# Two-layer decoder trunk on one core: background steps admitted by an account of VectorE's columns, a second W tile in PSUM, rotations and late gates on GpSimd

## The chip, the cores and the metric

The kernel runs on one core of a Trainium2 chip. The metric is the device time of one execution in microseconds; here the median of the runs shown. One execution was profiled; its trace gives the rows below.

## What is computed

Two decoder layers over 256 positions of width 2048, in float32, followed by an RMSNorm. Each layer normalizes its input, projects it with one wide matrix, runs several kinds of attention side by side (layer 0: latent attention with 8 heads, block-sparse attention with 8, attention into 256 memory tokens with 4; layer 1: sliding-window attention with sinks, 16 heads, dilated attention with 6, memory attention with 4), gates the concatenated heads with SiLU, projects back and adds the residual. Layer 0, cut to what matters:

```python
h = rms_norm(x, norm_g) @ w_in
c_q, c_kv, k_pe, qkv_b, q_mem, gate = split_cols(h, EVEN_SPLITS)
q_a = (rms_norm(c_q, q_norm_g) @ w_uq).reshape(B, S, MLA_HEADS, MLA_NOPE + MLA_ROPE)
q_a = jnp.concatenate([q_a[..., :MLA_NOPE], apply_rope(q_a[..., MLA_NOPE:], MLA_ROPE)], axis=-1)
...
y = jnp.concatenate([o_a, o_b.astype(o_a.dtype), o_m.astype(o_a.dtype)], axis=-1) * jax.nn.silu(gate)
return x + (y @ w_out).astype(x.dtype)
```

`apply_rope` rotates pairs of a head's first columns by an angle that grows with the position: x1\*cos - x2\*sin and x1\*sin + x2\*cos. These are "the rotations" below.

## The kernel before

**The stream of weights.** All weight matrices are cut into 334 pieces of 128 x 1024 columns at most, in a fixed plan (`_plan`): groups with names such as qr, kn0, v0, qn0, gB0 in layer 0, p0 to p9 in layer 1, and wo00 to wo13 for the output projections. A piece is loaded by a DMA (`raw`), rounded on ScalarE into `hi` (L393), and VectorE computes `lo = raw - hi` (L398). TensorE then does three passes per product, x_hi\*w_hi, x_hi\*w_lo, x_lo\*w_hi (L539 to L541): twelve matmuls of 128 x 512 for a full piece, in two halves of six. `raw`, `hi` and `lo` are rings of four tiles each (`RB`, `HB`); `ensure` runs three pieces ahead. A group's result stands in two of four `mm` banks of PSUM.

**The background.** Everything else is written as Python generators that emit a few instructions and then yield: evacuation of a group's banks (`rows`, by L663 to L675) into two tiles `wide`, rotation there (`rope_rows`, L592 to L621), a transposed layout by VectorE's 32x32 transposes (`g_land`, L634) and a round trip through DRAM, splits of queries and keys, scores, softmax (`g_softmax`), probabilities scaled into the tile `W` (L831, L832, L857, L859), transposed (`g_turn`, L812) and sent through DRAM, the product with the values, and the gate (`g_finish` L747 when the gate is there first, `g_gate` L764 when the head was first: a late gate). Results of layer y are split into columns of bufB or bufA, the input of the output projection.

**What sets the order.** Each engine runs its queue in the order in which instructions were emitted. `step` emits one piece: half of its matmuls, the late `lo` split of the piece two ahead, one round of background, the other half, the `hi` of the piece three ahead, one more round. A round is `run_bg`: each active generator advances by one yield, so by as many instructions as that step has; new heads start at most each fourth round, with six at once at most.

```python
        for g in list(active):
            try:
                next(g)
            except StopIteration:
                active.remove(g)
```

The attention banks (`at`) are four, handed out in turn, `W` is one tile, `wide` two. When a new group needs an `mm` bank whose evacuation has not been emitted, `mmtile` emits the rest of it on the spot (`force`).

## Time and profile before

| | |
|---|---|
| median of 3 runs | 991.64 us (991.05 to 991.83) |
| the profiled execution | 990.85 us, of which the span of instructions 989.1 us |
| mean granted TensorE clock | 0.992 |
| TensorE matmul busy | 965.4 us (98%) |
| VectorE busy | 696.2 us (70%) |
| ScalarE busy | 574.4 us (58%) |
| GpSimd busy | 20.0 us (2%) |
| chain that ended last | TensorE 87%, VectorE 7%, ScalarE 3% |

The profiled execution's own time is its span and 1.8 us around it. Busy time is an average over the whole span; where an engine waits is read from the waits and from the stretches. The granted clock is a share of TensorE's full speed: 1.00 is its upper level of 2.4 GHz, 0.50 the lower one of 1.2 GHz.

### The profile page before, as it was taken

Reading aid. Unit: us, or ns where it says so; the run is one execution under the profiler, and the core shown is the slowest. Engines: PE = TensorE matmul, PEld = TensorE weight load, DVE = VectorE, ACT = ScalarE, POOL = GpSimd, SP = SyncE. Lnnn points to the kernel's source line nnn. Section 1 sums busy time; section 2 is a strip of 40 time slices with the busy share of each in tenths; the row PEclk is TensorE's granted clock in tenths of the full one; section 3 lists DMA queues with packets and bytes.
Section 4 is the critical chain, followed back from the end, with each engine's and each line's share of the span. In section 5 each row is a group of like instructions: output and inputs, shape, how many; then the busy total and the mean of one; then the engine's idle time right before and its main releaser. Section 6 shows DMA issues by size and latency. Waiting matters only on the chain.

```text
span 989.1 us, 13362 instructions
## 1 busy us (share of the span) xinstructions
PE 965.4 (98%) x4541; PEld 808.9 (82%) x4541; DVE 696.2 (70%) x1324; ACT 574.4 (58%) x1045; POOL 20.0 (2%) x27
## 2 busy tenths in 40 slices
PE   9999998999999999999999999999898999999996
PEld 7888787888888888888888888887686988898885
DVE  6646879888567657776657656877888776786743
ACT  7766656676545646655556444655665664564541
POOL 0001000000000000000000000000000000000310
PEclk9999998999999999999999999999999999999998
DMA  8888978897767677888978756777766887688832
GB/s 332 323 278 267 304 228 268 272 310 229 238 215 245 216 240 246 266 280 269 331 249 289 261 195 218 236 234 235 251 220 212 269 274 227 217 296 301 288 125 85
DMA packets 136691, 248.25 MB, mean 251 GB/s; under 512 B 38960, under 2 KB 80176, under 8 KB 136624
## 3 DMA queue, kind: packets, MB, share of 16 engines
q1 hardware_dynamic: 135904, 246.59, 75.4%
q10 hardware_dynamic: 720, 0.82, 0.2%
q8 instruction: 35, 0.57, 0.2%
q14 instruction: 32, 0.26, 0.1%
HBM read 216.05 MB, written 31.33 MB: 250 GB/s over the span
## 4 chain that ended last, share of the span: by engine, by line
PE 87%; DVE 7%; ACT 3%; DMA 1%; issue 1%; SPq 0%; POOL 0%; DVEq 0%; ACTq 0%
PE mm L540 27%; PE mm L539 27%; PE mm L541 26%; PE at L917 2%; DVE lo L398 2%; PE at L908 2%; ACT hi L393 1%; PE at L912 1%; PE mm L1499 1%; PE mm L1498 1%; PE mm L1497 1%; DMA big<-in_memT 1%; DVE e L606 1%; DVE big L634 1%; DMA raw<-in_wall 1%
## 5 line engine op out<-in xcount | busy, mean ns | idle before, releaser
L398 DVE TENSOR_TENSOR lo<-raw,hi 128x1024 fp32r<-128x1024 f32 (+3 forms) x329 | 393.8, 1201 | 188.7 <-ACT hi L393 187.6
L393 ACT ACTIVATE hi<-raw 128x1024 fp32r<-128x1024 f32 (+3 forms) x329 | 339.2, 1035 | 219.3 <-PE mm L541 171.8
L540 PE MATMUL mm<-lo,bufB 128*128 128x512 f32 (+1 forms) x680 | 264.7, 389 | 7.0 <-DVE lo L398 6.9
L539 PE MATMUL mm<-hi,bufB 128*128 128x512 f32 (+1 forms) x680 | 265.8, 391 | 4.3 <-ACT wide L587 3.9
L541 PE MATMUL mm<-hi,bufB 128*128 128x512 f32 (+1 forms) x680 | 263.7, 388 | 0.0
L540 PE MATMUL mm<-lo,bufA 128*128 128x512 f32 (+1 forms) x620 | 239.3, 386 | 2.5 <-DVE lo L398 2.5
L539 PE MATMUL mm<-hi,bufA 128*128 128x512 f32 (+1 forms) x620 | 239.9, 387 | 0.6 <-DVE wide L583 0.6
L541 PE MATMUL mm<-hi,bufA 128*128 128x512 f32 (+1 forms) x620 | 238.8, 385 | 0.0
L540 PEld LDWEIGHTS mm<-lo,bufB 128*128 128x128 f32 x680 | 129.2, 190 | 33.4 <-DVE lo L398 9.1
L539 PEld LDWEIGHTS mm<-hi,bufB 128*128 128x128 f32 x680 | 129.3, 190 | 29.8 <-ACT wide L587 4.1
L541 PEld LDWEIGHTS mm<-hi,bufB 128*128 128x128 f32 x680 | 129.0, 190 | 24.6
L540 PEld LDWEIGHTS mm<-lo,bufA 128*128 128x128 f32 x620 | 116.5, 188 | 25.7 <-DVE lo L398 3.8
L539 PEld LDWEIGHTS mm<-hi,bufA 128*128 128x128 f32 x620 | 116.4, 188 | 23.2 <-PE mm L541 1.0
L541 PEld LDWEIGHTS mm<-hi,bufA 128*128 128x128 f32 x620 | 116.4, 188 | 23.1
L799 ACT ACTIVATE P<-P,st 128x128 f32<-128x128 f32 x76 | 33.7, 445 | 19.9 <-DVE st L793 18.9
L634 DVE STREAM_TRANSPOSE big<-wide 128x512 f32<-128x512 f32 (+1 forms) x68 | 43.5, 677 | 0.0
L790 DVE CUSTOM_DVE_ANT_1 P<-at,lay 128x128 f32<-128x128 f32 x76 | 24.0, 353 | 25.3 <-PE at L908 25.2
L831 ACT ACTIVATE W<-P,st 128x256 f32<-128x256 f32 x38 | 19.1, 502 | 26.9 <-DVE P L812 19.5
L812 DVE STREAM_TRANSPOSE P<-W 128x384 f32<-128x384 f32 (+1 forms) x54 | 28.7, 531 | 1.7 <-ACT W L831 1.5
L556 ACT ACTIVATE spl<-big 128x128 fp32r<-128x128 f32 (+1 forms) x76 | 23.5, 353 | 6.3 <-PE at L908 6.3
L843 ACT ACTIVATE PT<-P 128x256 fp32r<-128x256 f32 x38 | 15.2, 408 | 17.6 <-PE at L917 14.7
L558 DVE TENSOR_TENSOR spl<-big,spl 128x128 fp32r<-128x128 f32 (+1 forms) x76 | 23.7, 350 | 1.6 <-ACT spl L556 1.5
(166 smaller groups left out, 678.5 us busy)
## 6 DMA issues: line engine op xcount, KB each, us to landing
raw<-in_wall SPq DMA_DIRECT2D x309, 512.0 KB, 4.4
wd<-big SPq DMA_DIRECT2D x32, 512.0 KB, 5.1
big<-wd SPq DMA_DIRECT2D x32, 512.0 KB, 5.2
pd<-P SPq DMA_DIRECT2D x38, 192.0 KB, 4.4
P<-pd SPq DMA_DIRECT2D x38, 192.0 KB, 4.4
raw<-in_wall SPq DMA_DIRECT2D x16, 384.0 KB, 4.2
raw<-in_wall SPq DMA_DIRECT2D x8, 320.0 KB, 3.3
big<-in_xT SPq DMA_DIRECT2D x4, 512.0 KB, 6.3
```

The costliest lines, as they stand in the source:

```text
L393: nc.scalar.activation(hi[:, c], raw[:, c], AF.Copy)
L398: nc.vector.tensor_tensor(lo[:, c], raw[:, c], hi[:, c].bitcast(F32), op=OP.subtract)
L539: nc.tensor.matmul(p, xh, hi[:, w], start=kt == 0, stop=False, skip_group_check=True)
L540: nc.tensor.matmul(p, xh, lo[:, w], start=False, stop=False, skip_group_check=True)
L541: nc.tensor.matmul(p, xl, hi[:, w], start=False, stop=kt == g.kt - 1, skip_group_check=True)
L556: nc.scalar.activation(hi, src, AF.Copy)
L558: nc.vector.tensor_tensor(lo, src, hi.bitcast(F32), op=OP.subtract)
L634: nc.vector.transpose(L[:, w * t:w * t + w], Ws[t][:, 0:w])
L790: nc.vector.tensor_tensor_reduce(P, rows_of(sc[:, c], n), laid_out(mask, 3)[:, :, t:t + n], 1.0, -3.0e38, OP.add, OP.max, s[:, t:t + 1])
L799: nc.scalar.activation(P, rows_of(sc[:, c], 2) if mask is None else P, AF.Exp, bias=s[:, 2 + t:3 + t], scale=scale, accum_out=s[:, 4 + t:5 ...
L812: nc.vector.transpose(P[:, 0:128 * n], W)
L908: nc.tensor.matmul(o, q[:, a + q0:a + q0 + 128], k[:, b:b + 256], start=first and i == 0, stop=last and i == 2, skip_group_check=True)
```

## The change

- **An account** (`Meter`, `SHARE`, `SAVED`). All VectorE instructions are emitted through `vec`, which adds 100 and the columns of the output to a sum. A round of background earns 720, and at most 1400 is kept; each generator's step is charged what it emitted on VectorE. When the balance is below zero, a generator is passed over in this round, unless it is the evacuation of a group (`urgent`).
- **W**: a second tile, in PSUM; the attention banks are three instead of four.
- **Rotations** (`rope_rows`) are emitted on GpSimd instead of VectorE: 112 instructions. **Late gates** (`g_gate`) too: 20 products; there are 20 instead of 23, three heads find their gate already there. The tiles `y` are handed out (`ys`) instead of taken in turn.
- **Evacuation**: the second tile's plain copies in `rows`, 18 in all, go to ScalarE instead of VectorE.

The diff, without the lines where `nc.vector` alone becomes `vec`:

```diff
@@ -28,6 +28,8 @@
 XIN, XSQ, MSQ = 9, 16, 24
 LEAD = 32
 WAIT = 10
+
+SHARE, SAVED = 720, 1400
 NLAND = 8
 
 
...
@@ -186,10 +188,26 @@
     return c
 
 
+class Meter:
+
+
+    def __init__(self, engine):
+        self.engine, self.spent = engine, 0
+
+    def __getattr__(self, name):
+        f = getattr(self.engine, name)
+
+        def call(out, *a, **k):
+            self.spent += 100 + int(np.prod(out.shape[1:]))
+            return f(out, *a, **k)
+        return call
+
+
 @with_exitstack
 def body(ctx, tc, xr, xT, memT, memr, wall, gains, fing, sinks, consts, out):
     nc = tc.nc
     plan = _plan()
+    vec = Meter(nc.vector)
 
     pers = ctx.enter_context(tc.tile_pool(name="pers", bufs=1))
     wp = ctx.enter_context(tc.tile_pool(name="wp", bufs=1))
...
@@ -240,10 +258,12 @@
     osg = qk
     pp = Free("P", 8, [128, 384], work)
     ptp = Free("PT", 3, [128, 512], work, F32R)
-    banks = Free("at", 4, [128, 512], ps)
+    banks = Free("at", 3, [128, 512], ps)
     x1d = dram.tile([4, 128, 1024], F32, name="x1d")
     pw = Free("W", 1, [128, 384], work)
+    pw.put(ps.tile([128, 512], F32, name="W1"))
     wide = Free("wide", 2, [128, 512], work)
+    ys = Free("y", 2, [128, 256], work)
     qf = Free("qf", 4, [128, 128], work)
     pds = Free("pd", 8, [128 * 384], dram)
     wds = Free("wd", 4, [256 * 512], dram)
...
@@ -429,7 +449,8 @@
 
 
     active, queue = [], deque()
-    ctl = {"i": 0, "gap": 0, "pace": 4, "max": 6, "heads": 0, "tick": 0, "meet": -1}
+    ctl = {"i": 0, "gap": 0, "pace": 4, "max": 6, "heads": 0, "tick": 0, "meet": -1, "share": 0}
+    urgent = set()
 
     def launch(g):
         active.append(g)
...
@@ -457,11 +478,17 @@
         if queue and ctl["heads"] < ctl["max"] and ctl["gap"] >= ctl["pace"]:
             active.append(head(queue.popleft()))
             ctl["gap"] = 0
+        ctl["share"] = min(ctl["share"] + SHARE, SAVED)
         for g in list(active):
+            if ctl["share"] < 0 and g not in urgent:
+                continue
+            spent = vec.spent
             try:
                 next(g)
             except StopIteration:
                 active.remove(g)
+                urgent.discard(g)
+            ctl["share"] -= vec.spent - spent
 
     mmring = deque()
 
...
@@ -503,6 +530,7 @@
             later.pop(0)()
         for g in done:
             launch(g)
+            urgent.add(g)
         run_bg()
         done = []
         halves(*splits[i], 1, done)
...
@@ -603,7 +632,7 @@
                   [:, :, 0:g] for i in range(2))
         e = wtile("e", 512, 2)
         A, B = (e[:, 256 * i:256 * i + 4 * g * m].rearrange("p (b g i) -> p b g i", b=4, i=m) for i in range(2))
-        mul, add = (lambda o, a, b: nc.vector.tensor_tensor(o, a, b, op=OP.mult)), OP.add
+        mul, add = (lambda o, a, b: nc.gpsimd.tensor_tensor(o, a, b, op=OP.mult)), OP.add
         if kind == "r":
             e = wtile("e", 512, 2)
             C, E = (e[:, 256 * i:256 * i + 4 * g * m].rearrange("p (b g i) -> p b g i", b=4, i=m) for i in range(2))
...
@@ -611,14 +640,14 @@
             mul(B, x2, sn)
             mul(C, x2, cs)
             mul(E, x1, sn)
-            nc.vector.tensor_tensor(x1, A, B, op=OP.subtract)
-            nc.vector.tensor_tensor(x2, C, E, op=OP.add)
+            nc.gpsimd.tensor_tensor(x1, A, B, op=OP.subtract)
+            nc.gpsimd.tensor_tensor(x2, C, E, op=OP.add)
         else:
             lo, hi = slice(0, m // 2), slice(m // 2, m)
             mul(A, v, cs)
             mul(B[:, :, :, lo], v[:, :, :, hi], sn[:, :, :, lo])
             mul(B[:, :, :, hi], v[:, :, :, lo], sn[:, :, :, hi])
-            nc.vector.tensor_tensor(v, A, B, op=OP.add)
+            nc.gpsimd.tensor_tensor(v, A, B, op=OP.add)
 
     def g_land(Ws, n, ropes, done, L=None):
 
...
@@ -663,28 +692,28 @@
                 o = laid_out(Ws[t], n)
                 src = rows_of(cur[t][:, 0:128 * n], n)
                 if n0:
-                    copy(o[:, :, 0:n0], src[:, :, 0:n0], r, t, t == 1)
+                    copy(o[:, :, 0:n0], src[:, :, 0:n0], r, t)
...
@@ -737,14 +766,17 @@
     def put_y(kt, y):
         dst, done = Y["buf"][:, kt, :], Y["done"]
         yield from split(y, dst)
+        ys.put(y)
         done.add(kt)
 
     def g_finish(kt, po):
 
         if kt in SG:
+            while not ys.free:
+                yield
             sg = SG.pop(kt)
-            y = wtile("y", bufs=2)
-            nc.vector.tensor_tensor(y.rearrange("p (g j) -> p g j", j=32),
+            y = ys.get()
+            vec.tensor_tensor(y.rearrange("p (g j) -> p g j", j=32),
                                     po[:, 0:256].rearrange("p (g j) -> p g j", j=32), sg.v, op=OP.mult)
             sg.drop()
             banks.put(po)
...
@@ -759,9 +791,11 @@
     def g_gate(kt, sg):
 
         if kt in OT:
+            while not ys.free:
+                yield
             o = OT.pop(kt)
-            y = wtile("y", bufs=2)
-            nc.vector.tensor_tensor(y.rearrange("p (g j) -> p g j", j=32),
+            y = ys.get()
+            nc.gpsimd.tensor_tensor(y.rearrange("p (g j) -> p g j", j=32),
                                     o.rearrange("p (g j) -> p g j", j=32), sg.v, op=OP.mult)
             osg.put(o)
             sg.drop()
...
@@ -829,10 +863,10 @@
         w = pw.get()
         (_, p0), (_, p1) = cuts3(P)
         nc.scalar.activation(laid_out(w, 3)[:, :, 1:3], p1, AF.Copy, scale=r[:, 1:2])
-        nc.vector.tensor_scalar(laid_out(w, 3)[:, :, 0:1], p0, r[:, 0:1], None, op0=OP.mult)
+        vec.tensor_scalar(laid_out(w, 3)[:, :, 0:1], p0, r[:, 0:1], None, op0=OP.mult)
         yield
         pw.put(w)
-        yield from g_turn(P, w, 3)
+        yield from g_turn(P, w[:, 0:384], 3)
         while not ptp.free:
             yield
         PT = ptp.get()
```

In the changed kernel's listings every VectorE row bears the line of `Meter` (L202). The rows below are the instructions of one engine in the order of its queue, `x4` for four alike; wide_125 and wide_126 are the two tiles for rows 0 to 127 and 128 to 255, `big` the tile that a group lands in, P and W a head's probabilities, `e` scratch of the rotation.

VectorE in layer 1, while heads of p2 and the rotation of p4 are in work: the last twelve of the fifteen rows behind one `lo` split (the three in front of them are a split of y, a late gate and a transpose), up to and with the next. Before:

```order
L805 TENSOR_TENSOR st<-st 128x2
L806 RECIPROCAL st<-st 128x2
L805 TENSOR_TENSOR st<-st 128x2
L806 RECIPROCAL st<-st 128x2
L558 TENSOR_TENSOR bufA<-y,bufA 128x256
L606 TENSOR_TENSOR e<-wide_125,cst 128x64
L606 TENSOR_TENSOR e<-wide_125,cst 128x8x4 x2
L621 TENSOR_TENSOR wide_125<-e 128x4x2x8
L606 TENSOR_TENSOR e<-wide_126,cst 128x64
L606 TENSOR_TENSOR e<-wide_126,cst 128x8x4 x2
L621 TENSOR_TENSOR wide_126<-e 128x4x2x8
L398 TENSOR_TENSOR lo<-raw,hi 128x1024
```

In the change, at the place where p4 lands (big_100), from behind one split to the second split after it:

```order
L202 TENSOR_TENSOR st<-st 128x2
L202 RECIPROCAL st<-st 128x2
L202 TENSOR_TENSOR st<-st 128x2
L202 RECIPROCAL st<-st 128x2
L202 TENSOR_TENSOR bufA<-y_127,bufA 128x256
L202 STREAM_TRANSPOSE P_109<-W_124 128x384
L202 TENSOR_TENSOR lo<-raw,hi 128x1024
L202 TENSOR_TENSOR bufA<-y_128,bufA 128x256
L202 TENSOR_SCALAR W_123<-P_110,st 128x4x32
L202 STREAM_TRANSPOSE big_100<-wide_125 128x512
L202 STREAM_TRANSPOSE big_100<-wide_126 128x512
L202 TENSOR_TENSOR lo<-raw,hi 128x1024
```

The rotation (`e`, L606 and L621) is gone from the queue, the gates' product too, and a split comes after six rows and after four instead of after fourteen.

VectorE in layer 0, from the evacuation of group qr to that of kn0. Before:

```order
L606 TENSOR_TENSOR e<-wide_125,lay 128x256 x4
L614 TENSOR_TENSOR wide_125<-e 128x32x8
L615 TENSOR_TENSOR wide_125<-e 128x32x8
L606 TENSOR_TENSOR e<-wide_126,lay 128x256 x4
L614 TENSOR_TENSOR wide_126<-e 128x32x8
L615 TENSOR_TENSOR wide_126<-e 128x32x8
L812 STREAM_TRANSPOSE P_108<-W_124 128x256
L634 STREAM_TRANSPOSE big_100<-wide_125 128x512
L634 STREAM_TRANSPOSE big_100<-wide_126 128x512
L583 COPY wide_126<-mm 128x512
L398 TENSOR_TENSOR lo<-raw,hi 128x1024
```

In the change:

```order
L202 TENSOR_TENSOR lo<-raw,hi 128x1024
L202 TENSOR_REDUCE st<-at_119 128x2
L202 TENSOR_SCALAR st<-st 128x2
L202 TENSOR_TENSOR spl_106<-big_98,spl_106 128x256
L202 TENSOR_TENSOR spl_107<-big_94,spl_107 128x256
L202 STREAM_TRANSPOSE big_100<-wide_125 128x512
L202 STREAM_TRANSPOSE big_100<-wide_126 128x512
L202 TENSOR_TENSOR lo<-raw,hi 128x1024
```

The twelve instructions of the rotation are gone; the copies into wide_126 too; the transposes that land qr (big_100) follow two `spl` splits. The rotation stands in GpSimd's queue, alone:

```order
L635 TENSOR_TENSOR e<-wide_125,lay 128x256 x4
L643 TENSOR_TENSOR wide_125<-e 128x32x8
L644 TENSOR_TENSOR wide_125<-e 128x32x8
L635 TENSOR_TENSOR e<-wide_126,lay 128x256 x4
L643 TENSOR_TENSOR wide_126<-e 128x32x8
L644 TENSOR_TENSOR wide_126<-e 128x32x8
```

Each transpose of big_100 now follows GpSimd's last row on its tile instead of VectorE's own.

## Rows read from the trace of the kernel before

**Rows 1.** Page, part 1 (busy us, share) and part 2 (granted TensorE clock).

```profile
PE 965.4 (98%) x4541; PEld 808.9 (82%) x4541; DVE 696.2 (70%) x1324; ACT 574.4 (58%) x1045; POOL 20.0 (2%) x27
...
PEclk9999998999999999999999999999999999999998
```

**Rows 2.** Waits of TensorE, whole span: us in total, times, longest.

```profile
PE mm L540 <- DVE lo L398: 9.3, 7, 2.9
PE mm L539 <- ACT wide L587: 3.9, 1, 3.9
```

**Rows 3.** Busy time by stretch: start:end, length, engines, clock, DMA.

```profile
core 0: us, PE busy (x) PEld busy (x) DVE busy (x) ACT busy (x) POOL busy (x), PEclk, DMA share, GB/s
104.00:110.00 6.00, 5.53 (x24) 4.24 (x23) 5.60 (x8) 1.32 (x2) 0.00 (x0) 1.00 0.78 252
147.50:151.60 4.10, 0.19 (x3) 0.01 (x1) 3.97 (x10) 1.17 (x3) 0.00 (x0) 0.82 0.15 60
151.60:156.90 5.30, 5.30 (x13) 4.15 (x14) 5.26 (x10) 3.49 (x9) 0.00 (x0) 0.50 0.43 106
195.00:200.00 5.00, 4.43 (x21) 3.41 (x21) 4.96 (x10) 4.16 (x12) 0.00 (x0) 1.00 0.94 327
500.00:520.00 20.00, 20.00 (x90) 16.57 (x89) 10.66 (x10) 10.76 (x14) 0.00 (x0) 1.00 0.78 247
680.00:706.00 26.00, 22.56 (x109) 17.69 (x110) 22.01 (x66) 15.47 (x39) 0.00 (x0) 1.00 0.54 173
738.00:761.00 23.00, 19.59 (x91) 15.26 (x90) 21.47 (x75) 14.69 (x40) 0.00 (x0) 1.00 0.57 178
761.20:764.50 3.30, 3.30 (x10) 2.53 (x9) 2.94 (x4) 1.03 (x2) 0.00 (x0) 0.50 1.00 305
```

**Rows 4.** Timeline of VectorE, 746 to 760.5: start us, us, what.

```profile
749.22 1.22 DVE L398 TENSOR_TENSOR lo<-raw,hi 128x1024 fp32r<-128x1024 f32 x1
...
753.66 1.22 DVE L398 TENSOR_TENSOR lo<-raw,hi 128x1024 fp32r<-128x1024 f32 x1
...
757.00 1.30 DVE L634 STREAM_TRANSPOSE big<-wide 128x512 f32<-128x512 f32 x2
...
758.99 1.22 DVE L398 TENSOR_TENSOR lo<-raw,hi 128x1024 fp32r<-128x1024 f32 x1
```

**Rows 5.** Page, part 5: xcount, then busy us and mean ns.

```profile
L398 DVE TENSOR_TENSOR lo<-raw,hi 128x1024 fp32r<-128x1024 f32 (+3 forms) x329 | 393.8, 1201 | 188.7 <-ACT hi L393 187.6
L393 ACT ACTIVATE hi<-raw 128x1024 fp32r<-128x1024 f32 (+3 forms) x329 | 339.2, 1035 | 219.3 <-PE mm L541 171.8
```

**Rows 6.** Waits of ScalarE, whole span.

```profile
ACT W L831 <- DVE P L812: 19.5, 8, 4.0
```

**Rows 7.** Timelines of ScalarE, VectorE and TensorE, 140 to 152.3.

```profile
140.43 0.60 ACT L587 ACTIVATE wide<-mm 128x512 f32<-128x512 f32 x1 [1.25 <-DVE big L634]
...
143.35 0.75 DVE L558 TENSOR_TENSOR spl<-big,spl 128x256 fp32r<-128x256 f32 x2
...
145.61 1.43 DVE L606 TENSOR_TENSOR e<-wide,lay 128x256 f32<-128x256 f32 x4
...
150.24 1.26 DVE L634 STREAM_TRANSPOSE big<-wide 128x512 f32<-128x512 f32 x2
...
151.59 0.80 PE L539 MATMUL mm<-hi,bufB 128*128 128x512 f32 x1 [3.91 <-ACT wide L587]
```

**Rows 8.** Groups of VectorE by line and shape, columns as in rows 5.

```profile
L764 DVE TENSOR_TENSOR y<-qk,big 128x256 f32<-128x256 f32 x23 | 9.5, 418 | 0.3
```

**Rows 9.** Timelines of GpSimd and VectorE, 924.5 to 932 and at 958.

```profile
925.03 5.55 POOL L1344 TENSOR_TENSOR big<-big,big 128x256 f32<-128x256 f32 x4 [395.29 <-ACT e L705]
...
924.71 1.21 DVE L398 TENSOR_TENSOR lo<-raw,hi 128x1024 fp32r<-128x1024 f32 x1
...
926.54 1.76 DVE L398 TENSOR_TENSOR lo<-raw,hi 128x1024 fp32r<-128x1024 f32 x1 [0.62 <-ACT hi L393]
...
957.83 0.74 POOL L1344 TENSOR_TENSOR big<-big,big 128x256 f32<-128x256 f32 x1
```

More of the change, by code (lines that the diff above doesn't have):

```diff
@@ L512, in step @@
             launch(g)
+            urgent.add(g)
         run_bg()
@@ L582, in copy @@
         if vector and r is None:
[L583 removed]
+            vec.tensor_copy(o, p)
         elif vector:
[L585 removed]
+            vec.tensor_scalar(o, p, r[:, t:t + 1], None, op0=OP.mult)
         elif r is None:
@@ L633, in g_land @@
         for t in range(2):
-            nc.vector.transpose(L[:, w * t:w * t + w], Ws[t][:, 0:w])
+            vec.transpose(L[:, w * t:w * t + w], Ws[t][:, 0:w])
             wide.put(Ws[t])
@@ L672, in evac @@
                     o, src = laid_out(Ws[t], n), rows_of(cur[t][:, 0:128 * n], n)
-                    nc.vector.tensor_scalar(o[:, :, n0:n], o[:, :, n0:n], 1.0, hx[:, t:t + 1], op0=OP.add, op1=OP.mult)
-                    nc.vector.tensor_tensor(o[:, :, n0:n], o[:, :, n0:n], src[:, :, n0:n], op=OP.mult)
+                    vec.tensor_scalar(o[:, :, n0:n], o[:, :, n0:n], 1.0, hx[:, t:t + 1], op0=OP.add, op1=OP.mult)
+                    vec.tensor_tensor(o[:, :, n0:n], o[:, :, n0:n], src[:, :, n0:n], op=OP.mult)
                 yield
@@ L709, in g_rstd @@
         s = wtile("st", 8, 16)
-        nc.vector.tensor_reduce(s[:, 0:2], ss[:, :, 0:4], axis=mybir.AxisListType.X, op=OP.add)
+        vec.tensor_reduce(s[:, 0:2], ss[:, :, 0:4], axis=mybir.AxisListType.X, op=OP.add)
         yield from rsqrt(s, n, r)
@@ L804, in g_softmax @@
         if sink is not None:
-            nc.vector.tensor_tensor(s[:, 4:6], s[:, 4:6], s[:, 6:8], op=OP.add)
-        nc.vector.reciprocal(s[:, 6:8], s[:, 4:6])
+            vec.tensor_tensor(s[:, 4:6], s[:, 4:6], s[:, 6:8], op=OP.add)
+        vec.reciprocal(s[:, 6:8], s[:, 4:6])
         yield s[:, 6:8]
     def g_turn(P, W, n):
-        nc.vector.transpose(P[:, 0:128 * n], W)
+        vec.transpose(P[:, 0:128 * n], W)
         yield
@@ L844, in g_causal_T @@
         yield
-        nc.vector.tensor_tensor(parts[1], p[:, 0:2], parts[0].bitcast(F32), op=OP.subtract)
+        vec.tensor_tensor(parts[1], p[:, 0:2], parts[0].bitcast(F32), op=OP.subtract)
         yield
@@ L878, in g_mem_T @@
         for t in range(2):
-            nc.vector.tensor_tensor(parts[1][:, t], p[t], parts[0][:, t].bitcast(F32), op=OP.subtract)
+            vec.tensor_tensor(parts[1][:, t], p[t], parts[0][:, t].bitcast(F32), op=OP.subtract)
         yield
@@ L1105, in vm_split @@
             hi, lo = V.parts[t]
-            nc.vector.scalar_tensor_tensor(lo, src[t], rm[:, t:t + 1], hi.bitcast(F32), op0=OP.mult, op1=OP.subtract)
-    nc.vector.memset(ones, 1.0)
+            vec.scalar_tensor_tensor(lo, src[t], rm[:, t:t + 1], hi.bitcast(F32), op0=OP.mult, op1=OP.subtract)
+    vec.memset(ones, 1.0)
     nc.scalar.dma_start(gn, gains)
     w = spl.free[0][:, 0:128]
-    nc.vector.memset(w.bitcast(F32), 1.0)
+    vec.memset(w.bitcast(F32), 1.0)
     for i in range(10):
         a = ones if i < 7 else w
-        nc.tensor.matmul(banks.free[3][:, 0:128], a, a, start=True, stop=True)
+        nc.tensor.matmul(banks.free[2][:, 0:128], a, a, start=True, stop=True)
     nc.scalar.activation(warm, ones[:, 0:2], AF.Exp)
@@ L1328, in evac @@
             for t in range(2):
-                nc.vector.tensor_tensor(x[:, t, :], cur[t], x[:, t, :], op=OP.add)
+                vec.tensor_tensor(x[:, t, :], cur[t], x[:, t, :], op=OP.add)
             yield
@@ L1447, in g_last @@
         for c in (lo, hi):
-            nc.vector.tensor_tensor(x[:, c], p[:, c], x[:, c], op=OP.add)
+            vec.tensor_tensor(x[:, c], p[:, c], x[:, c], op=OP.add)
         nc.scalar.activation(q, x[:, lo], AF.Square, accum_out=ss[:, t, 3:4])
-        nc.vector.tensor_tensor_reduce(q1, x[:, hi], x[:, hi], 1.0, 0.0, OP.mult, OP.add, ss[:, t, 4:5])
-        nc.vector.tensor_reduce(s[:, 0:1], ss[:, t, :], axis=mybir.AxisListType.X, op=OP.add)
+        vec.tensor_tensor_reduce(q1, x[:, hi], x[:, hi], 1.0, 0.0, OP.mult, OP.add, ss[:, t, 4:5])
+        vec.tensor_reduce(s[:, 0:1], ss[:, t, :], axis=mybir.AxisListType.X, op=OP.add)
         yield
@@ L1454, in g_last @@
         nc.scalar.activation(b, a, AF.Sqrt, bias=eps, scale=1.0 / D)
-        nc.vector.tensor_scalar(v, a, 1.0 / D, EPS, op0=OP.mult, op1=OP.add)
+        vec.tensor_scalar(v, a, 1.0 / D, EPS, op0=OP.mult, op1=OP.add)
         yield
-        nc.vector.reciprocal(b, b)
-        nc.vector.scalar_tensor_tensor(u, b, v, b, op0=OP.mult, op1=OP.mult)
-        nc.vector.tensor_scalar(u, u, -0.5, 1.5, op0=OP.mult, op1=OP.add)
+        vec.reciprocal(b, b)
+        vec.scalar_tensor_tensor(u, b, v, b, op0=OP.mult, op1=OP.mult)
+        vec.tensor_scalar(u, u, -0.5, 1.5, op0=OP.mult, op1=OP.add)
         r = rx[:, t:t + 1]
-        nc.vector.tensor_tensor(r, u, b, op=OP.mult)
+        vec.tensor_tensor(r, u, b, op=OP.mult)
         yield
@@ L1472, in leave @@
             else:
-                nc.vector.tensor_scalar(o, o, r, None, op0=OP.mult)
-            (nc.sync if e is nc.vector else nc.scalar).dma_start(
+                vec.tensor_scalar(o, o, r, None, op0=OP.mult)
+            (nc.sync if e is vec else nc.scalar).dma_start(
                 out[j][:, 512 * t + c.start:512 * t + c.stop], o)
         full = slice(0, 512)
-        for j, c, e in ((0, lo, nc.vector), (0, hi, nc.vector), (1, full, nc.scalar), (3, full, nc.vector),
-                        (2, lo, nc.scalar), (2, hi, nc.vector)):
+        for j, c, e in ((0, lo, vec), (0, hi, vec), (1, full, nc.scalar), (3, full, vec),
+                        (2, lo, nc.scalar), (2, hi, vec)):
             leave(j, c, e)
```

54 lines of the change are left out of this document (26 added, 28 removed).

## The prediction

> **What bounds the kernel now.** I read the page first. TensorE is busy for 98% of the span and holds the granted clock in nearly every slice [rows 1]. So the time is TensorE's own stream plus its gaps, and a change elsewhere can win only gaps and half-clock time. Next, TensorE's waits over the whole execution: 9.3 us in seven waits for a `lo` split of VectorE, and 3.9 us in a single wait for an evacuation into `wide` on ScalarE [rows 2]. Then the stretches [rows 3]. TensorE's idle time is span minus busy: 0.47 us at 104 to 110, 3.91 us at 147.5 to 151.6, 0.57 us at 195 to 200, 3.44 us at 680 to 706, 3.41 us at 738 to 761. Behind two gaps the granted clock is 0.50, TensorE's lower level of 1.2 GHz, for 5.3 and 3.3 us. Undisturbed, at 500 to 520, 90 matmuls take 20.00 us, which is 0.222 each and 2.67 us for a piece of twelve.
>
> Why the `lo` splits are late is seen on VectorE's timeline in layer 1 [rows 4]: three consecutive splits start at 749.22, 753.66 and 758.99. Between them lie 4.44 and 5.33 us, where TensorE wants a piece each 2.67 us. The gap is full of background work, each row short, that the emitter put between two splits. The reserve is what the ring of four hi/lo pairs gives: a split may start when TensorE has left the piece four before it, and is wanted three pieces later, so 3 x 2.67 less 1.04 for `hi` and 1.20 for `lo` [rows 5], or 5.8 us. Two such intervals use up (4.44 + 5.33) - 2 x 2.67 = 4.4 us of it; a few in a row end it.
>
> ScalarE also loses 19.5 us in eight waits, the longest 4.0 us, for VectorE's transpose out of the single tile `W` [rows 6]; `hi` splits queue behind these waits.
>
> The wait at 151.59 is another thing. The groups kn0 and v0 are one piece each, so the group qn0 needs kn0's banks again 2 pieces later; those are emptied into `wide`, and `wide` is still held by the rotation of the group before (qr). VectorE's queue delays that rotation to 145.61, and the transposes that free `wide` start at 150.24 [rows 7].
>
> **The change, part by part.**
>
> *The account.* A half piece earns 720 units, so a piece 1440. A 128x256 operation counts 356 units and lasts 0.418 us [rows 8], so a piece gets about 1.69 us of background; with a split of 1.20 us VectorE then works 2.9 us per piece against 2.67 us and whatever attention matmuls the piece has. In the changed order at the same place of layer 1, six rows stand between the first two splits where there were fourteen; between the next two stand a 128x256 row (0.42), a smaller one (below 0.42) and two transposes (1.30, [rows 4]), with the split at most 3.4 us against 5.33. At that rate the reserve of 5.8 us isn't used up. I take both layer 1 stalls as gone: -3.44 - 3.41 = **-6.85 us**. With the second goes the half clock at 761.2 to 764.5, which does 1.65 us of work in 3.3: **-1.65 us**. The waits at 104 to 110 and 195 to 200 have the same cause, a split behind other VectorE work: -0.47 - 0.57 = **-1.04 us**. The rest of rows 2 (9.3 - 3.4 - 3.4 - 0.5, about 2.0 us before 95 us) stands at a place where the order does not change: 0.
>
> *Work delayed by the account* must still come in time. In the program's order the last gated column of layer 0 is split one piece ahead of its use (three before), that of layer 1 two (three before). One piece is 2.67 us, over the two 0.42 us operations and one split in front; I cost it at 0, and at up to 2.7 us if that cover fails.
>
> *The second W*, in PSUM, takes one attention bank. It frees ScalarE of much of the 19.5 us; this is off the path once splits are early: 0, and it makes the -6.85 safer. The price, three banks for four, is a rival below.
>
> *Copies of rows and columns.* Eighteen evacuation copies go from VectorE to ScalarE. ScalarE is at 58% and its `hi` splits have the reserve too: 0.
>
> *Late gates.* Twenty products go to GpSimd, at 0.74 us alone for 0.418 [rows 8, 9]. They have a piece or more to spare: 0.
>
> *Rotations.* All go to GpSimd. No row shows one there. The nearest is the 128x256 product: 0.74 us when VectorE runs no split [rows 9]. A 128x256 rotation step is the same shape, so 0.74; for 128 and 64 columns it is the upper bound, and in proportion to the columns 0.37 and 0.19. By contrast four such products during splits took 5.55 us, 1.39 each, and the split beside them 1.76 instead of 1.21 [rows 9]. The two engines hold each other up.
>
> At **qr** I work the chain through. In the new order one more split stands ahead of the transposes that free `wide` (+1.2), so ScalarE's copies, at 140.43 before, end at about 142.2 and 142.8. GpSimd takes 6 x 0.74 = 4.45 us per tile, and loses 1.97 us in the first to a split (1.22) and two `spl` rows (0.75, [rows 7]) that now run beside it: done at 148.6 and 153.1. A transpose is 0.65 and the copy that empties a bank of kn0 0.60: banks free at 149.9 and 154.3. TensorE comes at about 146.8 (one block of attention matmuls, 0.7 us, has moved behind this place), waits 3.1, does three matmuls, waits 3.7. That is 6.8 us for 3.91: **+2.9 us**. The half clock behind it stays. With every step at 1.39 us it would be 12 x 1.39 less the 10.9 above, 5.8 us worse; with the rotation done in VectorE's old time of 4.3 us but without its queue, the wait would vanish (-3.9, and -2.65 for 5.3 us of half clock).
>
> The GPSIMD Engine Reference of the Trainium skill (section Performance versus the Vector engine) gives two-input arithmetic as 1.96 times VectorE's time. By that an estimate of a step is 1.96 x 0.418 = 0.82 us, and the qr wait would be another 1.0 us longer; the row's 0.74 is used.
>
> At the ten other full rotations (two tiles, eight steps of 128 or 64 columns) the steps add up to between 2 x (0.37 + 0.19 + 0.19 + 0.37) = 2.2 and 8 x 0.74 = 5.9 us. The order leaves about a piece to a piece and a half, 2.7 to 4 us, before VectorE reaches the transposes, so VectorE stands still there for 0 to 3 us, less than the 5.8 us in reserve. I take **+1.0 us** in all, nearer the lower end, since most steps are of the small shapes; up to 10 if each place overruns by 1 us.
>
> **Sum:** -6.85 - 1.65 - 1.04 + 2.9 + 1.0 = -5.6 us. The profiled execution took 990.85 us (span 989.1), 0.8 under the median of the three runs, 991.64; it gives 985.2, the median **986.0 us**.
>
> **Rivals.**
>
> 1. *The qr wait goes too.* If GpSimd's steps are shorter than 0.74 us or meet no splits there, 3.9 us and 2.65 us of half clock go instead of +2.9: 986.0 - 9.4 = 976.6, call it 978. Against it: VectorE has two-input rows to run right there.
>
> 2. *GpSimd and VectorE hold each other up* (slower). Mechanism: each rotation step that meets a split pushes it from 1.21 to 1.76 us and is itself pushed to 1.39 [rows 9]; VectorE's transposes then wait on a late GpSimd with the next `lo` queued behind them, and TensorE behind that. It decides once an average step takes over about 0.9 us, when eight steps exceed the 4 us in the order plus a good part of the reserve. Price: qr 2.9 + 5.8, ten places 1 us over, and the layer 1 stalls, which lie among rotations, stay: -1.65 - 1.04 + 8.7 + 10 = +16 at the most; half of it gives 999.6. For it: 1.39 is measured, at splits back to back. Against: a VectorE that waits at a transpose runs no split, so GpSimd is alone and catches up. The Trainium skill's page SBUF — State Buffer (section SBUF: two separate sides) has it as a lock held for the whole instruction, between a GpSimd operation and a VectorE one with two SBUF inputs; the 1.76 us agrees with it.
>
> 3. *TensorE waits for a bank.* With three, the order has three places in layer 1's pair heads where a bank is handed on in the same half piece as its release. If VectorE's read is late by a split and a read (1.2 + 0.4), three such waits and a repeat are some 5 to 6 us, which eats the win: 991.5. Against it: no wait on a bank stands in rows 2, though two banks were handed on after one half piece before.
>
> 4. *The account does nothing for the time*, because evacuations are exempt and the rotation only trades places: about 991, part of the "same" below.
>
> **How the numbers follow.** Forecast (982 to 989.5): 0.52. Rival 1: 0.14. Rival 2: 0.20. Rivals 3 and 4: 0.14. A measurement of this kernel can tell about 0.2%, 2 us, from no change. Faster: 0.52 + 0.14 + 0.02 = 0.68; same 0.12; slower 0.20. The range takes in rival 1 and the lower half of rival 2: 977 to 995, leaving out some 0.03 below and 0.13 above.
>
> **What would show it.** Right: TensorE's waits for `lo` in layer 1 under 1 us together; one wait of 6 to 7 us, in two parts, at qr with ScalarE's `wide` named, itself behind a transpose; GpSimd busy about 70 to 110 us; VectorE some 35 us less busy. Wrong: waits of TensorE on `at` banks (rival 3); `lo` waits right behind rotations (rival 2); a gap at the start of an output projection (delayed work); or a qr wait under 2 us (rival 1).

## The result, and the profile after

The changed kernel took 981.95 us (median of 4 runs, 980.83 to 982.77) beside 991.35 us for the kernel before (median of 4, 990.03 to 991.83). The ratio is 0.9907, 95% interval 0.9889 to 0.9924: 9.4 us faster, where 5.6 were forecast. 986.0 was too high by 4 us, and 977 to 995 held the result; the band of the forecast itself, 982 to 989.5, was missed by 0.05 us at its lower end. The profiled execution took 980.83 us, 10.0 less than the one before.

The page of the changed kernel, part 1 (busy us, share, instructions), the granted clock, and the shares of the chain that ended last:

```profile
PE 960.9 (98%) x4541; PEld 806.7 (82%) x4541; DVE 665.8 (68%) x1174; ACT 584.4 (60%) x1060; POOL 95.5 (10%) x159
...
PEclk9999998999999999999999999999999999999999
...
PE 84%; DVE 0%; ACT 0%; POOL 0%; issue 0%; ACTq 0%; DVEq 0%
```

VectorE is 30 us less busy and GpSimd 76 us more [rows 1]: work that took VectorE 0.42 us or less per row takes GpSimd longer. VectorE's share of the chain fell from 7% to 0%. All waits of TensorE in the changed kernel (us in total, times, longest):

```profile
PE mm L568 <- ACT wide L616: 5.5, 2, 2.9
PE mm L569 <- DVE lo L202: 2.4, 3, 1.2
PE at L1149 <- DVE ones L202: 1.0, 1, 1.0
PE mm L568 <- ACT hi L389: 0.6, 1, 0.6
```

Matmuls of the weight stream go into `mm` banks, attention matmuls into `at` banks. Against [rows 2] the waits for `lo` fell from 9.3 us in seven to 2.4 in three, all before 95 us; the wait for `wide` grew from 3.9 to 5.5 and has two parts. Nothing waits for an attention bank (the row on `at` is the start, where `ones` is filled). The busy times by stretch of the changed kernel, columns as in [rows 3]:

```profile
104.00:110.00 6.00, 6.00 (x29) 4.95 (x28) 4.19 (x5) 2.23 (x3) 1.01 (x4) 1.00 1.00 303
140.00:160.00 20.00, 14.53 (x59) 11.13 (x58) 13.15 (x19) 10.98 (x21) 9.78 (x12) 0.83 0.56 174
149.00:155.80 6.80, 3.85 (x10) 2.55 (x9) 4.37 (x6) 3.43 (x8) 2.21 (x4) 0.50 0.26 62
195.00:200.00 5.00, 4.99 (x22) 3.80 (x21) 4.26 (x7) 5.00 (x12) 0.00 (x0) 1.00 0.97 271
600.00:800.00 200.00, 200.00 (x1000) 168.45 (x999) 149.22 (x322) 127.36 (x271) 23.67 (x46) 1.00 0.78 250
```

TensorE is idle for 5.47 us at 140 to 160 (20.00 less 14.53) and for no more than 0.05 us at a time anywhere else between 95 us and its last matmul; the 200 us at 600 to 800 hold no gap and no half clock. The kernel before is idle there for 6.86 us:

```profile
600.00:800.00 200.00, 193.14 (x967) 161.88 (x966) 154.71 (x376) 122.41 (x274) 0.00 (x0) 0.99 0.74 237
```

Where the time came from can be counted in TensorE's own stream: both traces hold the same 4,008 matmuls into `mm` banks in the same order. The n-th of them starts earlier than before by 0.19 us for the 100th (31 us), 0.96 for the 480th (113 us), 0.33 for the 2,500th (608 us) and 10.08 for the last. At each of these four equally many attention matmuls have gone before in both traces. So 0.77 us was won at 104 us, 0.63 net was lost from 113 to 608 us, which holds qr and the place at 195 us, and 9.75 was won in layer 1.

Around qr the timeline of the changed kernel reads (the rows of GpSimd, VectorE, ScalarE's copies and TensorE that matter; start us, us, what, idle before):

```profile
140.61 1.19 ACT L616 ACTIVATE wide<-mm 128x512 f32<-128x512 f32 x2 [2.38 <-DVE big L202]
...
141.35 3.79 POOL L635 TENSOR_TENSOR e<-wide,lay 128x256 f32<-128x256 f32 x4 [36.23 <-ACT wide L616]
...
142.78 1.77 DVE L202 TENSOR_TENSOR lo<-raw,hi 128x1024 fp32r<-128x1024 f32 x1 [1.67 <-ACT hi L413]
...
145.91 1.28 DVE L202 TENSOR_TENSOR spl<-big,spl 128x256 fp32r<-128x256 f32 x2
145.93 0.97 POOL L644 TENSOR_TENSOR wide<-e 128x256 f32<-128x256 f32 x1
146.86 2.94 POOL L635 TENSOR_TENSOR e<-wide,lay 128x256 f32<-128x256 f32 x4
147.10 0.70 DVE L202 STREAM_TRANSPOSE big<-wide 128x512 f32<-128x512 f32 x1
147.90 0.60 ACT L616 ACTIVATE wide<-mm 128x512 f32<-128x512 f32 x1 [3.58 <-DVE big L202]
...
148.55 0.50 PE L568 MATMUL mm<-hi,bufB 128*128 128x512 f32 x1 [2.53 <-ACT wide L616]
...
150.56 0.72 POOL L644 TENSOR_TENSOR wide<-e 128x256 f32<-128x256 f32 x1
151.32 0.71 DVE L202 STREAM_TRANSPOSE big<-wide 128x512 f32<-128x512 f32 x1 [3.52 <-POOL wide L644]
151.96 1.18 DVE L202 TENSOR_TENSOR lo<-raw,hi 128x1024 fp32r<-128x1024 f32 x1
152.13 0.60 ACT L616 ACTIVATE wide<-mm 128x512 f32<-128x512 f32 x1 [3.63 <-DVE big L202]
...
152.78 0.80 PE L568 MATMUL mm<-hi,bufB 128*128 128x512 f32 x1 [2.95 <-ACT wide L616]
```

It is the chain of the prediction, step for step: GpSimd's six steps, a transpose, a copy, TensorE, and the same again for the second tile. The first tile took GpSimd 5.55 us (141.35 to 146.90) where 6.42 were taken, the second 4.42 (4.45 taken).

### The profile page after: what moved, and what is told of

It reads as the page before. It is cut to its first block, busy times and chain, and to the rows that moved or that the text cites. A ratio compares the mean times of both kernels' runs of the same rounds, so it can differ in the third digit from the quotient of the medians.

```text
span 979.0 us, 13403 instructions
## 1 busy us (share of the span) xinstructions
PE 960.9 (98%) x4541; PEld 806.7 (82%) x4541; DVE 665.8 (68%) x1174; ACT 584.4 (60%) x1060; POOL 95.5 (10%) x159
## 4 chain that ended last, share of the span: by engine, by line
PE 84%; DVE 0%; ACT 0%; POOL 0%; issue 0%; ACTq 0%; DVEq 0%
PE mm L568 25%; PE mm L569 25%; PE mm L570 25%; PE at L951 2%; PE at L942 2%; PE at L946 1%; PE mm L1533 1%; PE mm L1532 1%; PE mm L1531 1%; PE at L955 1%; PE at L1069 0%; DVE big L202 0%; ACT big L1505 0%; DVE st L202 0%; POOL wide L644 0%; ACT wide L616 0%
## 5 line engine op out<-in xcount | busy, mean ns | idle before, releaser
L202 DVE TENSOR_TENSOR lo<-raw,hi 128x1024 fp32r<-128x1024 f32 (+3 forms) x331 | 398.9, 1211 | 187.0 <-ACT hi L413 184.3
L635 POOL TENSOR_TENSOR e<-wide,cst 128x64 f32<-128x64 f32 (+2 forms) x48 | 22.3, 491 | 284.1 <-ACT wide L618 143.8
L202 DVE STREAM_TRANSPOSE big<-wide 128x512 f32<-128x512 f32 (+1 forms) x68 | 44.0, 680 | 4.9 <-POOL wide L644 3.9
L798 POOL TENSOR_TENSOR y<-qk,big 128x256 f32<-128x256 f32 x20 | 19.1, 969 | 198.6 <-DMA big<-wd 139.4
L202 DVE CUSTOM_DVE_ANT_1 P<-at,lay 128x128 f32<-128x128 f32 x76 | 24.1, 354 | 20.1 <-PE at L942 20.0
L635 POOL TENSOR_TENSOR e<-wide,lay 128x64 f32<-128x64 f32 (+4 forms) x34 | 18.8, 581 | 148.1 <-ACT wide L618 111.8
```

The lines of the kernel that those rows point to most:

```text
L202: return f(out, *a, **k)
L635: mul, add = (lambda o, a, b: nc.gpsimd.tensor_tensor(o, a, b, op=OP.mult)), OP.add
L798: nc.gpsimd.tensor_tensor(y.rearrange("p (g j) -> p g j", j=32), o.rearrange("p (g j) -> p g j", j=32), sg.v, op=OP.mult)
```

## The experiments

Each time is the median beside the kernel before, measured on the same chip: 991.18 us for runs 1 to 4, 991.38 for runs 6 to 9, 990.51 for runs 5 and 10.

### 1. All of the change but the account

```diff
-SHARE, SAVED = 720, 1400
+SHARE, SAVED = 10**9, 10**9
```

> The changed kernel with the account switched off (a share so large that no step is ever passed over); second W, copies, rotations and gates as in the change. Theory A, the account carries the gain: the bursts between two lo splits come back, less the rotation and the gates that are now on GpSimd; TensorE's lo waits in layer 1 come back at half of 6.85 us or more, with the half clock behind them: 986 to 990 us. Theory B, taking work off VectorE carries it: the order hardly matters once 32 us of rotations and gates are gone; lo waits in layer 1 stay under 1 us: 981 to 983 us. In both the qr wait stays between 4 and 6.5 us.

Measured: 983.68 us, ratio 0.9929 (0.9915 to 0.9943). Neither theory holds. By stretch:

```profile
600.00:710.00 110.00, 109.61 (x522) 90.30 (x521) 77.94 (x158) 66.61 (x136) 10.48 (x20) 1.00 0.74 235
710.00:800.00 90.00, 88.14 (x481) 76.33 (x480) 72.65 (x186) 63.09 (x153) 12.81 (x27) 1.00 0.78 258
```

Of the 6.86 us idle in layer 1, 2.25 came back (0.39 and 1.86), and no half clock. So the rest of the change, without the account, does most of the work that the prediction gave to the account. Rotations, gates, copies and the second W went in together here; no run shows which of them does it without the account. What is left has this form, on VectorE's timeline:

```profile
751.15 0.71 DVE L202 STREAM_TRANSPOSE big<-wide 128x512 f32<-128x512 f32 x1 [1.21 <-POOL wide L650]
752.07 0.71 DVE L202 STREAM_TRANSPOSE big<-wide 128x512 f32<-128x512 f32 x1 [0.21 <-POOL wide L650]
752.71 1.00 DVE L202 STREAM_TRANSPOSE P<-W 128x384 f32<-128x384 f32 x2
753.63 2.32 DVE L202 TENSOR_TENSOR lo<-raw,hi 128x1024 fp32r<-128x1024 f32 x2
```

VectorE stands at the transposes of a group behind GpSimd's rotation for 1.21 and 0.21 us, with two `lo` splits behind them: rival 2's mechanism. At the other wait, at 698 us, it is the same: VectorE stood 2.21 and 0.85 us behind GpSimd, with the split behind. In the change the same two transposes, at 749.05, wait for nothing.

### 2. The account alone

The kernel before with `Meter` and the rule in `run_bg`; rotations, late gates and second-tile copies stay on VectorE and aren't charged.

```diff
+        ctl["share"] = min(ctl["share"] + SHARE, SAVED)
         for g in list(active):
+            if ctl["share"] < 0 and g not in urgent:
+                continue
```

> The kernel before with the account alone: rotations, gates and the copies of the second tile stay on VectorE and are not charged, one W, four banks. Theory A (the account carries the gain): the lo waits of layer 1 go (6.85 us and 1.65 of half clock), the qr wait stays near 3.9: 982 to 984 us. Theory B (work off VectorE carries it): the uncharged rotations still come in bursts, lo waits of 4 us or more stay in layer 1: 987 to 991 us.

Measured: 983.16 us, ratio 0.9926 (0.9911 to 0.9940), as theory A has it. VectorE is 694.7 us busy, as before the change, and yet:

```profile
600.00:710.00 110.00, 110.00 (x526) 91.04 (x525) 83.29 (x179) 65.59 (x133) 0.00 (x0) 1.00 0.73 230
710.00:800.00 90.00, 89.02 (x461) 75.79 (x460) 71.95 (x190) 56.67 (x131) 0.00 (x0) 1.00 0.79 257
```

0.98 us idle in place of 6.86. The wait at qr is 4.5 us, where 3.9 was expected. With run 1 this gives four corners: neither part about 991, either part about 983, both 982. The two parts, the account and all the rest, remove the same waits; their gains don't add.

### 3. Rotations back on VectorE

```diff
-        mul, add = (lambda o, a, b: nc.gpsimd.tensor_tensor(o, a, b, op=OP.mult)), OP.add
+        mul, add = (lambda o, a, b: nc.vector.tensor_tensor(o, a, b, op=OP.mult)), OP.add
```

and so for the sums and differences of `rope_rows`.

> The changed kernel with the 112 rotation steps back on VectorE, not charged to the account. Theory A: the qr wait falls from 5.5 to about 4 us, since the twelve steps take 4.3 us on VectorE against 9.9 on GpSimd, and a few lo waits of under 1 us come back: 980 to 983 us. Theory B: lo waits come back in layer 1 by 4 us or more, as VectorE has its 31 us of steps again: 986 to 990 us.

Measured: 982.76 us, ratio 0.9919 (0.9907 to 0.9931): theory A's time, not its reason at qr. Layer 1 is idle for 0.55 us. The wait at qr was to fall to 4 us and is one of 5.1, so GpSimd isn't the main reason for its length: VectorE's queue, with the twelve steps in it, comes to both transposes at 150.37, where in the change they start at 147.10 and 151.32 (this execution is 0.7 us behind at that place).

### 4. One W and four banks again

```diff
-    banks = Free("at", 3, [128, 512], ps)
+    banks = Free("at", 4, [128, 512], ps)
...
-    pw.put(ps.tile([128, 512], F32, name="W1"))
```

> The changed kernel with one W and four attention banks again. Theory (the second W is off the path): ScalarE's wait for W comes back, some 10 to 20 us in all, and the time stays within 1 us of the change, 981 to 983. Rival (it carries part of the gain, because hi splits queue behind that wait and lo splits behind them): lo waits of 2 us or more on TensorE, 984 to 987. Rival the other way (three banks cost something that no wait names): 979 to 980.5.

Measured: 982.27 us, ratio 0.9914 (0.9900 to 0.9927). The waits of ScalarE for `W` are back, 18.0 us in the three lines below against 6.5 in the change, and TensorE is idle for 0.00 us from 600 to 800. With the account at work, the second W and the bank that it takes come to nothing together.

```profile
ACT W L890 <- DVE P L202: 7.0, 5, 2.1
ACT W L864 <- DVE P L202: 5.7, 5, 1.6
ACT W L864 <- DVE st L202: 5.3, 9, 1.3
```

### 5. Gates and copies back on VectorE

```diff
-            nc.gpsimd.tensor_tensor(y.rearrange("p (g j) -> p g j", j=32),
+            nc.vector.tensor_tensor(y.rearrange("p (g j) -> p g j", j=32),
...
-                    copy(o[:, :, 0:n0], src[:, :, 0:n0], r, t)
+                    copy(o[:, :, 0:n0], src[:, :, 0:n0], r, t, t == 1)
```

> The changed kernel with the twenty late gates and the eighteen copies of second tiles back on VectorE, not charged to the account; rotations stay on GpSimd. Theory (both are off the path, as the prediction costs them at 0): 981.5 to 983 us, lo waits in layer 1 under 1 us. Rival (it was ScalarE's faster evacuation or the gates' absence from VectorE that emptied its queue): lo waits of 2 us or more in layer 1, 984 us or above.

Measured: 981.99 us, ratio 0.9916 (0.9899 to 0.9932). Layer 1 has no idle time, as the theory has it: both are off the path.

### 6. More work for GpSimd

```diff
-            mul(A, v, cs)
-            mul(B[:, :, :, lo], v[:, :, :, hi], sn[:, :, :, lo])
-            mul(B[:, :, :, hi], v[:, :, :, lo], sn[:, :, :, hi])
+            for _ in range(2):
+                mul(A, v, cs)
+                mul(B[:, :, :, lo], v[:, :, :, hi], sn[:, :, :, lo])
+                mul(B[:, :, :, hi], v[:, :, :, lo], sn[:, :, :, hi])
```

> The changed kernel with the three products of each d and c rotation step emitted twice on GpSimd (the second writes the same values): fourteen steps of about 0.54 us per group where there were eight, 7.6 us for 4.3; qr as it is. Theory (the order and the reserve of 5.8 us cover GpSimd up to about 8 us per group): VectorE stands at the transposes 3 to 4 us per group, TensorE's lo waits rise by 0 to 3 us: 981.5 to 985. Rival 2 of the prediction (VectorE behind a late GpSimd passes it on to TensorE at once): 1 us or more at each of ten groups: 990 or above.

Measured: 982.19 us, ratio 0.9911 (0.9895 to 0.9928). GpSimd's groups of the `d` and `c` rotations, in the change and here (the third row of each also holds eight products of qr and eight of ckv's position columns, which are not doubled):

```profile
L635 POOL TENSOR_TENSOR e<-wide,cst 128x64 f32<-128x64 f32 (+2 forms) x48 | 22.3, 491 | 284.1 <-ACT wide L618 143.8 <-issue 123.4 <-DVE st L202 16.9
L650 POOL TENSOR_TENSOR wide<-e 128x128 f32<-128x128 f32 (+2 forms) x22 | 10.7, 488 | 1.7
L635 POOL TENSOR_TENSOR e<-wide,lay 128x64 f32<-128x64 f32 (+4 forms) x34 | 18.8, 581 | 148.1 <-ACT wide L618 111.8 <-ACT wide L616 36.2
```

```profile
L635 POOL TENSOR_TENSOR e<-wide,cst 128x64 f32<-128x64 f32 (+2 forms) x96 | 39.1, 441 | 272.2 <-ACT wide L618 148.3 <-issue 123.9
L651 POOL TENSOR_TENSOR wide<-e 128x128 f32<-128x128 f32 (+2 forms) x22 | 12.5, 569 | 1.7
L635 POOL TENSOR_TENSOR e<-wide,lay 128x64 f32<-128x64 f32 (+4 forms) x52 | 25.2, 516 | 148.1 <-ACT wide L618 111.8 <-ACT wide L616 36.2
```

And VectorE's wait for them here:

```profile
DVE big L202 <- POOL wide L651: 13.8, 11, 1.9
```

That is 25.0 us more (76.8 less 51.8) over eleven rotations (p4 has two), 2.3 us each. VectorE now stands behind GpSimd eleven times, 13.8 us in all and 1.9 at the longest, against 0.8 us in the change. TensorE is idle for 0.00 us from 600 to 800: the reserve of four pieces takes it up. The step that rival 2 named as the point of decision, 0.9 us on average, wasn't reached even so; where it lies wasn't tried.

### 7. The rotation of qr on two engines

The second tile's six steps go to VectorE, their scratch to a free `big` tile.

```diff
-        e = wtile("e", 512, 2)
+        eng = nc.vector if kind == "r" and t else nc.gpsimd
+        e = big.free[0][:, 0:512] if eng is nc.vector else wtile("e", 512, 2)
```

> The changed kernel; at qr alone the six steps on the second tile (wide_126) go to VectorE, with their scratch in a free big tile, those on the first stay on GpSimd. Theory (the qr wait is GpSimd's twelve steps one behind the other, 9.9 us): the second part of the wait, 2.9 us, goes; the first, 2.7 us, stays, since the first tile still ends at about 147 on GpSimd: one wait of 2.5 to 3.2 us, 978.5 to 979.5 us. Rival (VectorE and GpSimd hold each other up): the steps on both engines take 1.2 us or more each, VectorE's lo split and the transposes come later, and the wait stays at 5 us or more: 982 to 984.

Measured: 981.22 us, ratio 0.9903 (0.9885 to 0.9922): not told from the change, and between the theory's range and the rival's. The wait isn't much shorter; its two parts became one of 5.1 us. On VectorE:

```profile
145.14 3.03 DVE L636 TENSOR_TENSOR big<-wide,lay 128x256 f32<-128x256 f32 x4
...
148.21 0.42 DVE L644 TENSOR_TENSOR wide<-big 128x256 f32<-128x256 f32 x1
...
150.35 1.30 DVE L202 STREAM_TRANSPOSE big<-wide 128x512 f32<-128x512 f32 x2
```

The steps stand in VectorE's queue behind a split and ahead of four more rows, so both transposes begin at 150.35, where the first began at 147.10 in the change (this execution is 0.7 us behind at that place); and beside GpSimd the four products take 0.76 us each, where VectorE alone took 0.36 in the kernel before [rows 7]. The theory had looked at GpSimd's chain and not at what the steps push back on VectorE.

### 8. A spare tile for kn0

Group kn0 is evacuated into a free `big` tile when both `wide` are held.

```diff
-            while len(wide.free) < 2:
+            while len(wide.free) < 2 and not (spare and big.free):
                 yield
+            B = None if len(wide.free) == 2 else big.get()
...
-        run(f"kn{g}", ckv, rows("pppp", lambda p, g=g: KN.update({g: p})))
+        run(f"kn{g}", ckv, rows("pppp", lambda p, g=g: KN.update({g: p}), spare=not g))
```

> The changed kernel; group kn0 is evacuated into a free big tile when the two wide tiles are held, so that its banks don't wait for qr's rotation. Theory (the wait is for wide alone): TensorE's wait for ScalarE's wide copies at qr, 5.5 us, goes; VectorE still stands at the transposes behind GpSimd until 151.3 with a lo split behind them, wanted at about 151.2 and ready at about 153, so a lo wait of 1.5 to 2.5 us takes its place; part of the 3.4 us of half clock goes: 975 to 979 us. Rival (the evacuation is late for ScalarE's own queue): the wait for wide stays at 3 us or more, 980 us or above.

Measured: 978.82 us, ratio 0.9876 (0.9853 to 0.9898). At 140 to 160 TensorE is idle for 1.61 us in place of 5.47, the `lo` wait that was expected behind the transposes, and the granted clock stays at 1.00. The theory held, in the wait and in the time. But 3.1 us of idle time stands at 160 to 205, where the change has 0.01 in its first profile and 0.61 in its second (run 10).

### 9. Spare tile and two engines together

> Both of the two edits before: kn0 into a free big tile, and the second tile's rotation at qr on VectorE. Theory: neither the wait for wide nor the lo wait behind the transposes is left, and with them goes the half clock behind qr (6.8 us at half speed, worth 3.4): 972.5 to 975 us. Rival (the half clock has another cause than the wait): 976 to 977 us with the granted clock at 0.50 for some microseconds near 150.

Measured: 978.39 us, ratio 0.9871 (0.9852 to 0.9891). The first half came: 0.47 us idle at 140 to 160, clock 1.00. The time (972.5 to 975 expected) didn't, for the next group set waits in its turn. By the matmuls of the stream this kernel is ahead of the change's first profile by 7.2 us at the 680th (168 us; 5.0 of idle time and about 1.9 of half clock, where 3.4 was expected of the clock, since TensorE stands still in part of that time) and by 3.0 from the 800th (198 us) to the end. By stretch:

```profile
140.00:160.00 20.00, 19.53 (x94) 15.93 (x92) 18.12 (x32) 13.99 (x29) 5.48 (x6) 1.00 0.61 180
160.00:205.00 45.00, 41.59 (x195) 33.71 (x194) 35.46 (x62) 26.44 (x50) 0.00 (x0) 1.00 1.00 329
```

and on TensorE's timeline:

```profile
183.52 0.47 PE L568 MATMUL mm<-hi,bufB 128*128 128x512 f32 x1 [1.33 <-DVE wide L202]
...
188.46 0.50 PE L568 MATMUL mm<-hi,bufB 128*128 128x512 f32 x1 [1.54 <-ACT wide L616]
```

At 183.52 kn1 wants the banks of gB0, whose evacuation stood on ScalarE behind a `hi` split that waited 5.26 us for its weights and a split of probabilities that waited 1.05 for its own load; at 188.46 v1 wants those of qn1, whose copies wait for `wide`. In the change's first profile TensorE came 7 us later and found both done; in its second (run 10) it still waited 0.26 us for the copies.

### 10. A spare tile for qn1 too, and the change once more

```diff
-            run(f"qn{g}", cq, rows("pppp", lambda p: launch(g_heads(g, V, p))))
+            run(f"qn{g}", cq, rows("pppp", lambda p: launch(g_heads(g, V, p)), spare=2 * g))
```

where 2 means a `big` tile in any case.

> The kernel with kn0 in a spare big tile and the split rotation at qr (978.39 us), and qn1 evacuated into a spare big tile too. Theory (with the wait at qr gone, the next one is the same thing one group set later: v1's matmuls at 188.5 us wait 1.54 us for qn1's copies, and these for the transposes that free wide): that wait goes, the 1.3 us behind the evacuation of gB0 at 183.5 stays: 976.5 to 977.2 us. Rival (ScalarE's queue, not wide, holds the copies): no change, 978 to 979.

> The changed kernel itself, beside its variants on one chip: 981 to 983 us. It tells whether the 3.6 us between it and the kernel with kn0 in a spare tile and the split rotation are more than the spread between chips.

Measured: 976.30 us, ratio 0.9860 (0.9843 to 0.9876), 0.2 us under the theory's range, and the change itself on this chip 982.28, ratio 0.9915 (0.9899 to 0.9931). The intervals don't touch: 6.0 us better than the change, 14.2 better than before. The wait for ScalarE's `wide` is gone from the list:

```profile
PE mm L569 <- DVE lo L202: 2.8, 4, 1.2
PE mm L568 <- DVE wide L202: 1.7, 2, 1.5
PE at L1153 <- DVE ones L202: 1.0, 1, 1.0
PE mm L568 <- ACT hi L389: 0.4, 1, 0.4
```

What TensorE still waits for on this path is gB0's evacuation (1.7 us), a `lo` split at 151 us (0.5 us) and what stands before 95 us.

## Why the prediction came out as it did

The direction and the two largest places were right, the largest term had its cause put too narrowly, and the sum was 4.5 us short. By the prediction's own terms, in profiled executions (from the lead in the stream of matmuls, above; the place at 195 us from the idle time there, 0.56 to 0.01 at 160 to 205, and qr as what remains of 113 to 608 us: 0.63 + 0.55). The last column is the same for the second profile of the change (run 10):

| term | predicted | measured | in run 10 |
|---|---|---|---|
| layer 1, waits and half clock | -8.5 | -9.75 | -9.75 |
| waits at 104 and 195 us | -1.04 | -0.77 - 0.55 = -1.3 | -0.81 + 0.05 = -0.8 |
| qr | +2.9 | +1.2 | +2.6 |
| ten other rotations | +1.0 | 0 | 0 |
| start | 0 | -0.2 | -0.4 |
| sum | -5.6 | -10.1 | -8.3 |

So layer 1 and the ten rotations are out by the same in both profiles, and qr by a figure that changes from one execution to the next.

**Layer 1** was sized by idle time. A matmul's row lasts 0.39 us while the next starts 0.23 us after it, so each gap counts some 0.16 us short in a table of busy time. From start to start, beyond the usual pace, the four gaps of the kernel before come to 3.06 + 0.71 + 1.26 + 2.47 = 7.50 us, where 6.85 were idle. With 1.7 us of half clock that is 9.2; the last 0.5 lies in no wait that the profile names. The cause was put wrong in part: the prediction gave the term to the account, and runs 1 and 2 show that the rest of the change alone does most of it (2.25 us idle left) and the account alone too (0.98 left). That the stalls stood only a little above the reserve of 5.8 us, so that either part takes them below it, would explain this; no run measures it. Nor is it settled what the account adds on top of the moved work. Without it VectorE comes to landings before GpSimd has done, and both waits left in run 1 stand behind such a place; but run 6, with the account, has eleven such places, 13.8 us in all, and TensorE doesn't wait.

**104 and 195 us.** The prediction gave both to a late split. At 104 us it is one, and it goes with the rotations: runs 2 and 3, which have them on VectorE, wait 0.47 us there, run 1 doesn't. At 195 us the kernel before waits for VectorE's copy of the second tile into `wide`:

```profile
PE mm L539 <- DVE wide L583: 0.6, 1, 0.6
```

This wait isn't reliably gone. In run 10 TensorE is idle there for 0.35 us, at the same matmul of the stream, now for ScalarE's copy, and for 0.26 us twelve matmuls earlier; most variants wait there too. The 0.55 of the table is one execution's.

**qr**: +2.9 predicted, +1.2 found in the first profile. The wait was 5.5 us for 6.8: GpSimd lost 1.1 us and not 1.97 to VectorE in the first tile (5.55 less 4.45). (ScalarE's copies and TensorE both came about 1 us earlier than taken, which cancels.) The other part is "the half clock behind it stays", which was taken as the same cost. The low level lasted from 149.0 to 155.8, as long as before, but TensorE stood still in nearly half of it: it worked 3.85 us at 0.50 where it had worked 5.3 [rows 3], 0.7 us less lost. That isn't the same in each execution: in run 10 the low level lasted 10.2 us, which costs some 1.5 us more, and qr comes to +2.6, close to the forecast. So part of this miss lies in the execution that was profiled, and not in the chain that was worked out. The 0.74 us per step held: the four products of the second tile, with VectorE at a transpose and then standing still, took 2.94 us. The Trainium skill's GPSIMD Engine Reference (section Performance versus the Vector engine) would give 0.82 by its ratio of 1.96; the measurement decides for 0.735.

**The ten rotations** cost nothing. GpSimd's 112 steps took 57.3 us, 0.51 each on the mean, between the bounds of 0.19 to 0.37 and 0.74 that the shapes gave; outside qr VectorE waited 0.8 us for those of `d` and `c`, and TensorE not at all. Run 6 shows that 2.3 us more per rotation would still have cost nothing, so the +1.0 was a price for something that the reserve covers. It was the prediction's own argument ("less than the 5.8 us in reserve") and should have been followed to 0.

**At 0** were the second W, the copies, the gates and the delayed work. Runs 4 and 5 show the first three at 0 (the gates even though they took GpSimd 0.97 us each, where 0.74 was taken), and no gap stands at an output projection.

**The rivals.** Rival 1 fell: the wait at qr is there. Rival 2 exists as a mechanism (run 1) but not at a size that decides. Rival 3 fell: no wait for a bank with three, and nothing won with four banks and one W. Rival 4 fell: the account alone gives 8 us.

## What to carry to other kernels

Two remedies for the same stall need not add up: measure each alone before paying for all (here, with the account and the rotations in place, the second W, the gates and the copies bought nothing). The wait for a tile that two groups share was cured here by another tile and not by another engine: a spare tile for kn0 gave 2.4 us more than the split of the rotation on the same chip (runs 8 and 7, whose times don't overlap), and the next wait stood one group set further on. Size a stall from start to start of the stalled engine's instructions, since idle time in a table of busy time counts each gap short.
